# Up products of two SwiGLU layers: the two parts of an operand laid side by side, so that a third of the matmuls are twice as wide

## The chip, the cores and the metric

The kernel runs on one core of one Trainium2 chip. Its time is the device time of one launch in microseconds (us), and smaller is better. A launch computes the whole block for one sequence; the host only lays the arrays out.

## The reference, cut to what matters

The input is `x` of 512 tokens by 1024 features, in fp32. The block is a SwiGLU layer, a mixer, and another SwiGLU layer, each behind an RMS norm and each added to `x`:

```python
def swiglu(x, w_gu, w_down):
    g, u = jnp.split(x @ w_gu, 2, axis=-1)     # w_gu is 1024 x 5632
    return (jax.nn.silu(g) * u) @ w_down       # w_down is 2816 x 1024

x = x + 0.5 * swiglu(rmsnorm(x, norm_ffn1_g), ffn1_w_gu, ffn1_w_down)
x = x + hybrid_mixer(rmsnorm(x, norm_mix_g), ...)
x = x + 0.5 * swiglu(rmsnorm(x, norm_ffn2_g), ffn2_w_gu, ffn2_w_down)
return rmsnorm(x, final_norm_g)
```

The change concerns `x @ w_gu` (the up product) in both SwiGLU layers and nothing else of the arithmetic.

## The kernel before, in words

**Precision.** Every fp32 operand is split in a high part, which is the operand rounded to the type fp32r, and a low part, which is the rest. A product of two operands is the sum of three matmuls: high weights by high activations, high weights by low activations, low weights by high activations.

**Weights.** All weight blocks come from one flat array in the order `PLAN`; `STEPS` is the order in which they are used. `Weights.issue` handles one step: a cast on ScalarE makes the high part `wh` (L331), a subtraction on VectorE makes the low part `wl` (L332), and transfers that add in memory (`f<-f`, L309, issued by GpSimd) and one VectorE addition a set (L318) form sums of blocks for later steps. `wh` and `wl` have three buffers each. `take` issues two steps ahead of the product that runs.

**The up product in sets.** The up product of a layer gives 22 pieces of 128 columns of `g` and as many of `u`. The first four of each are done plainly (`mm_group`, `mm_single`, L380 and L366), and in each layer nine sets of seven products follow (`run_sets`, `Set.run`, L502). A set computes, with sums and differences of blocks (a Winograd scheme), a 2 by 2 block product with seven products instead of eight: its rows are the `g` and `u` columns, its columns are the two halves of 256 tokens (`HW`). The products are called m1, p2, q6, p5, q7, p4, p3. The order of two neighbouring sets s and t is written out in `order`: s.q6, s.p5, s.q7, t.m1, s.p4, t.p2, s.p3, t.q6 and so on. `Operands.make` splits the activation operand of each of the seven products once a layer, in 14 buffers of the pool `op`; its results stay for all nine sets.

**One product** is 24 matmuls: three terms, four 128-row pieces of the contraction, two 128-column pieces `e` of the weights. Each takes 128 x 128 weights and 256 columns of activations, and adds into one bank of PSUM of 512 fp32 a partition: columns 0 to 255 for `e` = 0, 256 to 511 for `e` = 1. A set has three banks: `b` takes m1, q6, q7, p4 one on top of the other; `a` starts as a copy of m1 (L507, ScalarE) and takes p2; `c` takes p5 and p3. After m1, q6 and q7 ScalarE copies the bank out (L510 for q6 and q7), and PE may go on adding to it when the copy is done; in the order above one other product always lies between. The results: after p2 a Silu of `a` (L727), after q7 `c` and the q7 copy together (L730), after p4 one half of the hidden tile (L734), after p3 `c` and the q6 copy (L739), Silu (L740) and the other half (L476).

**PSUM** has eight banks a core. Here six go round under the tag `mm`, two under `aux`. In the second SwiGLU layer `natural(i)` turns eight 128 x 512 pieces of `x`, one after the p3 of each of the first eight sets, with four 128 x 128 transposes on PE into an `aux` bank (L771) and a copy by ScalarE (L772).

**Order.** Which instruction stands where in an engine's queue is planned when the kernel is built, by priority (the program's order) and by when the planner takes an operand to be ready; at run time each engine goes through its queue in that order. Only the last stretch is scheduled by hand. After the sets `down_product` begins (`natural_set`, L625); its operands are split while the last sets run (L600, L601, L579, L583).

Of the kernel before, what the change touches and what calls it, by code (L numbers as in the profile page):

```python
# [12 lines left out]
ALU = mybir.AluOpType  # L13
# [166 lines left out]
def block_kernel(ctx: ExitStack, tc: tile.TileContext, xT, vecs, gf, gup, wgl, wts, out):  # L180
# [6 lines left out]
    ps = ctx.enter_context(tc.tile_pool(name="ps", bufs=6, space=bass.MemoryType.PSUM))  # L187
    pa = ctx.enter_context(tc.tile_pool(name="pa", bufs=2, space=bass.MemoryType.PSUM))

    cnt = [0]  # L190

# [10 lines left out]
    def tile_of(pool, shape, dtype=F32):  # L202
        cnt[0] += 1
        return pools[pool].tile(shape, dtype, tag=pool, name=f"{pool}{cnt[0]}")

    def T(dtype=F32):
        return tile_of("tp", [P, S], dtype)

    def MM():
        cnt[0] += 1  # L210
        return ps.tile([P, S], F32, tag="mm", name=f"mm{cnt[0]}")

    def AUX():
        cnt[0] += 1
        return pa.tile([P, S], F32, tag="aux", name=f"aux{cnt[0]}")


    ones = front.tile([P, P], F32, tag="ones", name="ones")
# [20 lines left out]
    class Weights:  # L239
# [239 lines left out]
    class Set:  # L479
# [34 lines left out]
        def first(self):  # L514
# [4 lines left out]
            nc.vector.tensor_tensor(out=t, in0=self.bank["a"], in1=self.v["m1"], op=ALU.add)  # L519
            return t  # L520

    class Operands:

        ORDER = ("m1", "p2", "p5", "q6", "q7", "p4", "p3")

        def __init__(self, b):
            self.b = b
            self.parts = {}  # L530
            self.sums = set()

# [19 lines left out]
        def make(self, p):  # L552
            if p in self.parts:
                return
            i = self.ORDER.index(p)
            if i > 0:
                self.make(self.ORDER[i - 1])
            v = self.sum(p)
            h, l = (tile_of("op", [P, 1024], F32R) for _ in range(2))
            hv, lv = (t.rearrange("p (k t) -> p k t", t=HW) for t in (h, l))  # L560
            nc.scalar.copy(hv, v)
            nc.vector.tensor_tensor(out=lv, in0=v, in1=hv.bitcast(F32), op=ALU.subtract)
            self.parts[p] = (h, l)
# [40 lines left out]
        def get(self, p):  # L604
            return self.parts[p]

    def natural_set(ops, banks, done, ahead=1):

        used = {"a"}
        for at, p in enumerate(SEQ):  # L610
            for q in SEQ[at : at + ahead + 1]:
                ops.make(q)
            n = {"m1": "b", "p2": "a", "q6": "b", "p5": "c", "q7": "b", "p4": "b", "p3": "c"}[p]
            fresh = n not in used
            used.add(n)
            o = banks[n]
            bh, bl = ops.get(p)
            for u in range(2):
                h, l = W.take()
                for j, (ww, aa) in enumerate(((h, bh), (h, bl), (l, bh))):  # L620
                    for i in range(2):
                        k = 2 * u + i
                        for t in range(2):
                            s = slice(k * HW + t * P, k * HW + (t + 1) * P)
                            nc.tensor.matmul(o[t], aa[:, s], ww[:, i * 512 : (i + 1) * 512],  # L625
                                             start=fresh and j == k == 0,
                                             stop=j == 2 and k == 3, skip_group_check=True)
            done(p, o)
# [21 lines left out]
    def ffn(up, down, norm, nxt, plain, at):  # L650
        xh, xl = norm.h, norm.l
        rows = []

        def finish(k):
            if k == at:
                rows.append(norm.finish())

        o = mm_group(up, KD, (0, DFF, P, DFF + P), xh, xl, extra=finish, slow=nxt is not None)
        row = rows[0]
        xn, xn_tile = {}, []  # L660

        def normed(j, l):

            if (j, l) not in xn:
                t = slice(l * HW, (l + 1) * HW)
                if not xn:
                    xn_tile.append(tile_of("hidw", [P, 4, 4, HW]))
                v = xn_tile[0][:, len(xn)]
                for i in range(4):
                    k = 4 * j + i  # L670
                    nc.vector.scalar_tensor_tensor(
                        out=v[:, i], in0=x[k][:, t],
                        scalar=vec[:, norm.goff + k : norm.goff + k + 1], in1=row[:, t],
                        op0=ALU.mult, op1=ALU.mult)
                xn[j, l] = v
            return xn[j, l]

        xo = Operands(normed)
# [36 lines left out]

        def down_operands(w):
            return DownOperands(
                lambda j, l: wides[w][:, 4 * j : 4 * j + 4, l * HW : (l + 1) * HW])

        def up_set(i):  # L720
            h = new_hid()

            def done(s, p):
                bank, v = s.bank, s.v
                if p == "p2":
                    s.g1 = T()
                    nc.scalar.activation(s.g1, s.first(), AF.Silu)  # L727
                if p == "q7":
                    u2 = T()
                    nc.vector.scalar_tensor_tensor(out=u2, in0=bank["c"], scalar=-1.0, in1=v["q7"],  # L730
                                                   op0=ALU.mult, op1=ALU.subtract)
                    s.u2 = u2
                if p == "p4":
                    nc.vector.scalar_tensor_tensor(  # L734
                        out=h[:, :, :HW], in0=pair(bank["b"]), scalar=-1.0, in1=pair(s.g1),
                        op0=ALU.mult, op1=ALU.mult)
                if p == "p3":
                    g2 = T()
                    nc.vector.tensor_tensor(out=g2, in0=bank["c"], in1=v["q6"], op=ALU.add)  # L739
                    nc.scalar.activation(g2, g2, AF.Silu)  # L740
                    mul(h[:, :, HW:], pair(s.u2), pair(g2))
                    if nxt is None and i < KD:
                        natural(i)
# [7 lines left out]
        def pair(t):  # L751
            return t.rearrange("p (e t) -> p e t", t=HW)

        run_sets(up_set)

        def split_hid(k):

            h, l = (tile_of("op", [P, 2, S], F32R) for _ in range(2))
            t = hid[k // 2]
            nc.scalar.copy(h, t)  # L760
            nc.vector.tensor_tensor(out=l, in0=t, in1=h.bitcast(F32), op=ALU.subtract)
            return h, l

        down_product(full(down, KF), split_hid, downs, nxt)

    def natural(i):

        X = XS[-1]
        o = AUX()
        for t in range(NTB):  # L770
            nc.tensor.transpose(o[:, t * P : (t + 1) * P], X[:, i, t * P : (t + 1) * P], ident)  # L771
        nc.scalar.copy(X[:, i], o)  # L772

    def down_product(us, split_hid, downs, nxt):
# [26 lines left out]
        A = [MM(), MM()]  # L801

        def run_wide(w):
            banks = {"a": A, "b": [(MM, AUX)[w % 2]() for _ in range(2)], "c": [MM(), MM()]}

            def done(p, o):
                for t in range(2):
# [10 lines left out]
                    elif p == "p3" and w < WIDE - 1:  # L818
                        add(0, 1, t, o[t], 0.5)

            natural_set(downs[w], banks, done)
            return banks["c"]

        for w in range(WIDE):
            C = run_wide(w)
# [728 lines left out]
```

## Time and profile before

| what | value |
|---|---|
| three runs | 1181.78, 1181.72, 1180.69 us; median 1181.72 |
| the profiled execution | 1180.99 us, of which 1179.3 us are the span of the trace |
| up products in sets, first layer | 50.15 to 231.58 us of the span |
| up products in sets, second layer | 878.47 to 1063.37 us |

The span is from the first to the last instruction of the trace; the profiled execution's own time is 1.7 us longer. Busy times of PE are modelled ends of pipelined matmuls, so what counts is the distance from one matmul's start to the next. PEld is the weight load of the same engine. In a group's row stand its count, its busy time, the mean of one in nanoseconds, then the idle time of the engine ahead of it and who ended that.

### The profile page before, as it was taken

The numbers are of one execution on the slowest core, as the hardware profiler recorded it, in microseconds if no ns is written. First come the engines' busy times: TensorE is split into PE (matmuls) and PEld (weight loads), VectorE is DVE, ScalarE is ACT, GpSimd is POOL, SyncE is SP. The second block draws the span as 40 slices with busy tenths as digits, with TensorE's granted clock in tenths as the row PEclk, the third lists the DMA queues.
The fourth block names the chain that finished last, engine by engine and source line by source line (L and its number), as shares of the span: only waits on it lengthen the run. The fifth ranks groups of instructions, "written<-read, shape, count | busy, mean of one in ns | idle before, by whom it ended". The sixth has DMA issues, their size and how long they took to land.

```text
span 1179.3 us, 19168 instructions
## 1 busy us (share of the span) xinstructions
PE 1170.9 (99%) x7794; PEld 1080.7 (92%) x7794; DVE 868.9 (74%) x1027; ACT 634.3 (54%) x790; POOL 117.4 (10%) x153
## 2 busy tenths in 40 slices
PE   9999999999999999999999999999999999999997
PEld 8899999988888889999999998998889999998886
DVE  7985656896568965767697787685598566579955
ACT  6564455674435655565565576544355554566543
POOL 0010101101010111100110100000001111001100
PEclk9999999999999999999999999999999999999999
DMA  9388777678524388777677766531638767757721
GB/s 350 79 210 197 171 193 178 158 199 206 212 85 113 87 207 223 189 180 200 180 196 192 199 199 186 141 109 44 232 68 211 181 180 175 190 153 186 178 83 72
DMA packets 62600, 200.25 MB, mean 170 GB/s; under 512 B 6864, under 2 KB 13136, under 8 KB 62512
## 3 DMA queue, kind: packets, MB, share of 16 engines
q0 software_dynamic: 18784, 68.17, 31.7%
q1 hardware_dynamic: 39088, 126.37, 30.9%
q10 hardware_dynamic: 4640, 4.49, 1.1%
q8 instruction: 61, 1.00, 0.3%
q14 instruction: 27, 0.22, 0.1%
HBM read 124.55 MB, written 8.39 MB: 113 GB/s over the span
## 4 chain that ended last, share of the span: by engine, by line
PE 97%; ACT 1%; issue 1%; DVE 1%; ACTq 0%; POOL 0%; POOLq 0%
PE mm L502 53%; PE mm L625 12%; PE mm L366 11%; PE mm L380 7%; PE mm L838 4%; PE aux L625 4%; PE aux L838 1%; PE aux L1161 1%; PE aux L1142 1%; PE aux L1120 1%; PE aux L1164 0%; PE aux L224 0%; PE aux L1121 0%; PE mm L857 0%; PE aux L771 0%
## 5 line engine op out<-in xcount | busy, mean ns | idle before, releaser
L331 ACT CAST wh<-f 128x1024 fp32r<-128x1024 f32 (+1 forms) x341 | 356.2, 1047 | 406.3 <-PE mm L502 207.4
L332 DVE TENSOR_TENSOR wl<-f,wh 128x1024 fp32r<-128x1024 f32 (+1 forms) x341 | 413.3, 1217 | 154.1 <-ACT wh L331 141.3
L502 PE MATMUL mm<-op,wh 128*128 128x256 f32 x3584 | 471.1, 284 | 0.4 <-ACT mm L507 0.4
L502 PEld LDWEIGHTS mm<-op,wh 128*128 128x128 f32 x3584 | 447.9, 192 | 2.2 <-ACT mm L507 0.8
L502 PE MATMUL mm<-op,wl 128*128 128x256 f32 x1792 | 251.5, 283 | 0.0
L502 PEld LDWEIGHTS mm<-op,wl 128*128 128x128 f32 x1792 | 231.2, 192 | 0.1
L309 POOL DMA_DIRECT2D f<-f x126 | 108.9, 869 | 929.0 <-DVE wl L332 542.2
L625 PE MATMUL mm<-wh,op 128*128 128x512 f32 x432 | 106.9, 389 | 0.0
L625 PEld LDWEIGHTS mm<-wh,op 128*128 128x128 f32 x432 | 80.9, 188 | 16.7
L366 PE MATMUL mm<-op,wh 128*128 128x512 f32 x384 | 91.0, 389 | 0.0
L366 PEld LDWEIGHTS mm<-op,wh 128*128 128x128 f32 x384 | 72.0, 188 | 14.9
L380 PE MATMUL mm<-op,wh 128*128 128x512 f32 x256 | 64.2, 393 | 0.0
L625 PE MATMUL mm<-wl,op 128*128 128x512 f32 x216 | 57.7, 389 | 0.0
L380 PEld LDWEIGHTS mm<-op,wh 128*128 128x128 f32 x256 | 48.1, 189 | 10.3
L318 DVE TENSOR_TENSOR f<-f,f 128x1024 f32<-128x1024 f32 x42 | 51.3, 1222 | 0.8
L625 PEld LDWEIGHTS mm<-wl,op 128*128 128x128 f32 x216 | 40.6, 188 | 8.4
L366 PE MATMUL mm<-op,wl 128*128 128x512 f32 x192 | 47.4, 389 | 0.0
L366 PEld LDWEIGHTS mm<-op,wl 128*128 128x128 f32 x192 | 36.0, 188 | 7.5
L510 ACT COPY tp<-mm 128x512 f32<-128x512 f32 x68 | 39.6, 583 | 0.0
L601 DVE TENSOR_TENSOR op<-hidw,op 128x1024 fp32r<-128x1024 f32 x28 | 34.0, 1219 | 1.1 <-ACT op L600 1.0
L380 PE MATMUL mm<-op,wl 128*128 128x512 f32 x128 | 34.3, 389 | 0.0
L416 ACT ACTIVATE op<-X,vec 128x512 fp32r<-128x512 f32 x23 | 16.5, 719 | 31.8 <-DVE X L859 24.3
(269 smaller groups left out, 1042.5 us busy)
## 6 DMA issues: line engine op xcount, KB each, us to landing
f<-wts SPq DMA_DIRECT2D x219, 512.0 KB, 4.5
f<-f POOLq DMA_DIRECT2D x126, 512.0 KB, 5.3
X<-xT SPq DMA_DIRECT2D x8, 256.0 KB, 5.3
xs<-X POOLq DMA_DIRECT2D x8, 256.0 KB, 2.3
ga<-tp ACTq DMA_DIRECT2D x8, 256.0 KB, 3.2
gb<-tp ACTq DMA_DIRECT2D x8, 256.0 KB, 4.7
tp<-ga SPq DMA_DIRECT2D x8, 256.0 KB, 4.3
y<-tp SPq DMA_DIRECT2D x7, 256.0 KB, 2.3
```

The source lines that it names most:

```text
L309: return nc.gpsimd.dma_start(out_, a, accum_op=ALU.add).ins
L318: nc.vector.tensor_tensor(out=s3, in0=a11, in1=a21, op=ALU.add)
L331: self.cast = nc.scalar.copy(h[:, :w], raw[:, :w]).ins
L332: nc.vector.tensor_tensor(out=l[:, :w], in0=raw[:, :w], in1=h[:, :w].bitcast(F32), op=ALU.subtract)
L366: nc.tensor.matmul(o, w[:, i * P : (i + 1) * P], a[k], start=j == k == 0, stop=j == 2 and k == kt - 1)
L380: nc.tensor.matmul(o[c], w[:, s : s + P], a[k], start=k == 0 and j == 0, stop=k == kt - 1 and j == 2)
L416: nc.scalar.activation(xh[k], x[k], AF.Copy, scale=g)
L502: nc.tensor.matmul(to, ww[:, s], aa[:, t], start=fresh and k == 0 and e == 0 and j == 0, stop=k == 3 and j == 2, skip_group_check=True)
L510: nc.scalar.copy(v, o)
L601: nc.vector.tensor_tensor(out=lv, in0=v, in1=hv.bitcast(F32), op=ALU.subtract)
L625: nc.tensor.matmul(o[t], aa[:, s], ww[:, i * 512 : (i + 1) * 512], start=fresh and j == k == 0, stop=j == 2 and k == 3, skip_group_check=True)
L838: nc.tensor.matmul(o[t][e], b if j == 1 else a, wl if j == 2 else wh, start=k == K0 and e == 1 and j == 0, stop=k == KF - 1 and j == 2, sk ...
```

## The change

Seven of the nine sets of each layer (all but the first and the last) run a product as 8 wide matmuls (high weights by 512 columns: the high and the low part of the activations side by side) and then 8 narrow ones (low weights by the high part, 256 columns). The wide result needs a bank for each `e`, so each accumulator is a pair of banks: the left halves hold high x high plus low x high, the right halves hold high x low, and the sum of left and right is formed when the result is taken out. The first and the last set run the 24 narrow matmuls as before, in the first bank of their pairs.

- `Both` replaces the split of `Operands.make` in the two SwiGLU layers: the same two buffers an operand, filled by two copies and two subtractions of 128 x 512 rather than one each of 128 x 1024.
- `PairSet` replaces `Set` for the up products. The copies out of a pair: after m1 one copy of both banks to `a` (128 x 1024); after q6 and q7 two copies of 128 x 512 on ScalarE and one addition on VectorE; `onto` is two additions on VectorE where there was one; `whole` is a copy on ScalarE and an addition on VectorE, used after p2 (`a`) and p4 (`b`), where there was none.
- PSUM is four pairs with fixed names while the sets run: `x` for every `a`, and `w`, `z`, `y` in turn for `b` and `c`. `banks` closes the six and two banks before the sets and opens them again behind them.
- The transposes of `natural` move from behind p3 to behind p5, into the pair `x`. They are issued as matmuls with the transpose flag, with `start` on the first of four only.
- The sets of the mixer keep `Set` and its banks.

```diff
+    def banks(paired=False):
+        stage.close()
+        for n, b in (("pairs", 1),) if paired else (("mm", 6), ("aux", 2)):
+            cnt[0] += 1
+            pools[n] = stage.enter_context(tc.tile_pool(
+                name=f"{n}{cnt[0]}", bufs=b, space=bass.MemoryType.PSUM, reuse_waits="tile"))
...
+    class Both:
+        def __init__(self, v):
+            self.t = []
+            for i in range(2):
+                t = tile_of("op", [P, 2, 2, HW], F32R)
+                w = v[:, 2 * i : 2 * i + 2]
+                nc.scalar.copy(t[:, :, 0], w)
+                nc.vector.tensor_tensor(out=t[:, :, 1], in0=w, in1=t[:, :, 0].bitcast(F32),
+                                        op=ALU.subtract)
...
+    class PairSet:
+        BANK = {"m1": "b", "p2": "a", "q6": "b", "p5": "c", "q7": "b", "p4": "b", "p3": "c"}
+        def __init__(self, group_, done, i, merged):
...
+            self.tags = {"a": "x", "b": "wzy"[i % 3], "c": "ywz"[i % 3]}
...
+            def product(to, ww, aa):
+                nonlocal first
+                for k in range(4):
+                    for e in range(2):
+                        nc.tensor.matmul(to(e), ww[:, k * HW + e * P : k * HW + (e + 1) * P],
+                                         aa(k), start=first and k == 0 and (self.merged or e == 0),
+                                         stop=k == 3 and ww is l, skip_group_check=True)
+                first = False
+            if self.merged:
+                product(lambda e: o[:, e], h, x_.both)
+                product(lambda e: o[:, e, :HW], l, x_.high)
+            else:
+                half = self.flat(n)
+                for ww, aa in ((h, x_.high), (h, x_.low), (l, x_.high)):
+                    product(lambda e: half[:, e * HW : (e + 1) * HW], ww, aa)
+            if p == "m1" and self.forked:
+                a = self.open("a")
+                if self.merged:
+                    nc.scalar.copy(a, o)
+                else:
+                    nc.scalar.copy(a[:, 0], o[:, 0])
+            elif p in ("m1", "q6", "q7"):
+                self.taken(p, n)
...
+        def taken(self, p, n):
...
+            nc.scalar.copy(pair(v), self.left(n))
+            nc.scalar.copy(pair(r), self.right(n))
+            nc.vector.tensor_tensor(out=v, in0=v, in1=r, op=ALU.add)
+        def onto(self, n, t):
...
+            for part in (self.left(n), self.right(n)):
+                nc.vector.tensor_tensor(out=pair(t), in0=part, in1=pair(t), op=ALU.add)
+        def whole(self, n):
...
+            nc.scalar.copy(pair(t), self.right(n))
+            nc.vector.tensor_tensor(out=pair(t), in0=self.left(n), in1=pair(t), op=ALU.add)
...
             def done(s, p):
                 if p == "p2":
+                    if s.forked:
+                        g = s.whole("a")
+                        s.g1 = g if s.merged else T()
+                    else:
+                        s.g1 = g = s.m1
+                        s.onto("a", g)
+                    nc.scalar.activation(s.g1, g, AF.Silu)
+                if p == "p5" and nxt is None and i < KD:
+                    natural(i, MM2("x")[:, 0])
                 if p == "q7":
+                    s.onto("c", s.q7)
                 if p == "p4":
+                    t = s.whole("b")
                     nc.vector.scalar_tensor_tensor(out=h[:, :, :HW], in0=pair(t), ...)
                 if p == "p3":
+                    s.onto("c", s.q6)
+                    nc.scalar.activation(s.q6, s.q6, AF.Silu)
+                    nc.vector.scalar_tensor_tensor(out=h[:, :, HW:], in0=pair(s.q7), ...)
...
-            return Set(xo, done)
+            return PairSet(xo, done, i, i not in (0, (KF - plain) // 2 - 1))
+        banks(paired=True)
         run_sets(up_set)
+        banks()
...
-    def natural(i):
+    def natural(i, o):
         X = XS[-1]
-        o = AUX()
         for t in range(NTB):
-            nc.tensor.transpose(o[:, t * P : (t + 1) * P], X[:, i, t * P : (t + 1) * P], ident)
+            b = slice(t * P, (t + 1) * P)
+            nc.tensor.matmul(o[:, b], X[:, i, b], ident, start=t == 0, stop=t == NTB - 1,
+                             is_transpose=True, skip_group_check=True)
         nc.scalar.copy(X[:, i], o)
```

More of the change, by code (lines that the diff above doesn't have):

```diff
@@ L520, in first, with high, low, both @@
             return t
+    class Both:
[7 more added lines that the diff above has]
+                                        op=ALU.subtract)
+                self.t.append(t)
+        def high(self, k):
+            return self.t[k // 2][:, k % 2, 0]
+        def low(self, k):
+            return self.t[k // 2][:, k % 2, 1]
+        def both(self, k):
+            return self.t[k // 2][:, k % 2].rearrange("p a t -> p (a t)")
@@ new lines, in pair, with left, right, open @@
+    def pair(t):
+        return t.rearrange("p (e t) -> p e t", t=HW)
+    class PairSet:
+        BANK = {"m1": "b", "p2": "a", "q6": "b", "p5": "c", "q7": "b", "p4": "b", "p3": "c"}
+        def __init__(self, group_, done, i, merged):
+            self.merged = merged
+            self.group = group_
+            self.done = done
+            self.tags = {"a": "x", "b": "wzy"[i % 3], "c": "ywz"[i % 3]}
+            self.bank = {}
+        def left(self, n):
+            return self.bank[n][:, :, :HW]
+        def right(self, n):
+            return self.bank[n][:, :, HW:]
+        def open(self, n):
+            self.bank[n] = MM2(self.tags[n])
+            return self.bank[n]
+        def run(self, p):
+            n = self.BANK[p]
+            fresh = n not in self.bank
+            o = self.open(n) if fresh else self.bank[n]
+            x_ = self.group.get(p)
+            h, l = W.take()
+            first = fresh
+            def product(to, ww, aa):
[21 more added lines that the diff above has]
+                self.taken(p, n)
+            self.done(self, p)
+        def flat(self, n):
+            return self.bank[n][:, 0]
+        def taken(self, p, n):
+            v = T()
+            setattr(self, p, v)
+            if not self.merged:
+                nc.scalar.copy(v, self.flat(n))
+                return
+            r = T()
+            nc.scalar.copy(pair(v), self.left(n))
+            nc.scalar.copy(pair(r), self.right(n))
+            nc.vector.tensor_tensor(out=v, in0=v, in1=r, op=ALU.add)
+        def onto(self, n, t):
+            if not self.merged:
+                nc.vector.tensor_tensor(out=t, in0=self.flat(n), in1=t, op=ALU.add)
+                return
+            for part in (self.left(n), self.right(n)):
+                nc.vector.tensor_tensor(out=pair(t), in0=part, in1=pair(t), op=ALU.add)
+        def whole(self, n):
+            if not self.merged:
+                return self.flat(n)
+            t = T()
+            nc.scalar.copy(pair(t), self.right(n))
+            nc.vector.tensor_tensor(out=pair(t), in0=self.left(n), in1=pair(t), op=ALU.add)
+            return t
@@ L605, in get, with natural_set @@
             return self.parts[p]
-    def natural_set(ops, banks, done, ahead=1):
+    def natural_set(ops, bank, done, ahead=1):
         used = {"a"}
@@ L615, in natural_set @@
             used.add(n)
-            o = banks[n]
+            o = bank[n]
             bh, bl = ops.get(p)
@@ L676, in normed @@
             return xn[j, l]
-        xo = Operands(normed)
+        xo = Operands(normed, Both)
         hid = []
@@ L803, in run_wide @@
         def run_wide(w):
-            banks = {"a": A, "b": [(MM, AUX)[w % 2]() for _ in range(2)], "c": [MM(), MM()]}
+            bank = {"a": A, "b": [(MM, AUX)[w % 2]() for _ in range(2)], "c": [MM(), MM()]}
             def done(p, o):
@@ L819, in done @@
                         add(0, 1, t, o[t], 0.5)
-            natural_set(downs[w], banks, done)
-            return banks["c"]
+            natural_set(downs[w], bank, done)
+            return bank["c"]
         for w in range(WIDE):
```

39 lines of the change are left out of this document (18 added, 21 removed).

## The prediction

> **What bounds the kernel now.** I read the head of the page first, then the chain that ended last, then the up products by stretch, and at the end the order of single instructions there. The page:
>
> ```profile
> span 1179.3 us, 19168 instructions
> PE 1170.9 (99%) x7794; PEld 1080.7 (92%) x7794; DVE 868.9 (74%) x1027; ACT 634.3 (54%) x790; POOL 117.4 (10%) x153
> PEclk9999999999999999999999999999999999999999
> PE mm L502 53%; PE mm L625 12%; PE mm L366 11%; PE mm L380 7%; PE mm L838 4%; PE aux L625 4%; PE aux L838 1%; PE aux L1161 1%; PE aux L1142 1%; PE aux L1120 1%; PE aux L1164 0%; PE aux L224 0%; PE aux L1121 0%; PE mm L857 0%; PE aux L771 0%
> L502 PE MATMUL mm<-op,wh 128*128 128x256 f32 x3584 | 471.1, 284 | 0.4 <-ACT mm L507 0.4
> ```
>
> PE is busy throughout, at its full granted clock, and the sets (L502) are 53% of the chain with 0.4 us of idle time over the whole run. The chain in order of time shows the pace of the two shapes:
>
> ```profile
> 28.39 21.76 PE mm L366 x96
> 50.15 181.43 PE mm L502 x1512
> 231.58 38.11 PE mm L625 x168
> ...
> 878.47 25.92 PE mm L502 x216
> 904.82 20.16 PE mm L502 x168
> 1046.10 17.27 PE mm L502 x144
> ```
>
> A 256-column matmul takes 181.43 / 1512 = 120.0 ns, a 512-column one 21.76 / 96 = 226.7 ns. So the first layer's nine sets run back to back, at 20.16 us a set and 2.88 us a product. The 256 further columns cost 106.7 ns; what is left of the narrow matmul, 120.0 - 106.7 = 13.3 ns, is paid for each instruction whatever its width.
>
> **The change part by part.** *PE.* A merged product is 8 wide and 8 narrow matmuls: 8 x 226.7 + 8 x 120.0 = 2773 ns, against 24 x 120.0 = 2880. It saves 107 ns, which is eight times those 13.3 ns. Seven sets of seven products in two layers are 98 merged products: 98 x 0.1067 = 10.5 us, all of it on the chain. A set goes from 20.16 to 19.41 us, so 0.75 us a set is what everything else may eat before nothing is left.
>
> The page TensorE: Matmul & The Clock Gate of the Trainium skill, section Back-to-back issue gap, gives warm matmuls as N / 2.4 + 2.5 ns, that is about 109 and 216 ns. By it the fixed part is 2.5 ns, the saving an estimated 8 x 2.5 = 20 ns a product and 2 us in all. The trace disagrees: 13.3 ns.
>
> *VectorE and ScalarE.* A steady set of the first layer, and the groups in it:
>
> ```profile
> 107.58:127.74 20.16, 20.16 (x171) 20.16 (x170) 12.20 (x12) 10.02 (x13) 2.57 (x3) 1.00 0.76 183
> L331 ACT CAST wh<-f 128x1024 fp32r<-128x1024 f32 x8 | 8.4, 1048 | 10.8 <-PE mm L502 9.5 <-issue 1.3
> L510 ACT COPY tp<-mm 128x512 f32<-128x512 f32 x2 | 1.2, 584 | 0.0
> L507 ACT COPY mm<-mm 128x512 f32<-128x512 f32 x1 | 0.6, 575 | 0.0
> L332 DVE TENSOR_TENSOR wl<-f,wh 128x1024 fp32r<-128x1024 f32 x7 | 8.6, 1223 | 4.9 <-ACT wh L331 4.9
> L318 DVE TENSOR_TENSOR f<-f,f 128x1024 f32<-128x1024 f32 x1 | 1.2, 1225 | 0.0
> L739 DVE TENSOR_TENSOR tp<-mm,tp 128x512 f32<-128x512 f32 x1 | 0.7, 693 | 1.5 <-PE mm L502 1.5
> L740 ACT ACTIVATE tp<-tp 128x512 f32<-128x512 f32 x1 | 0.6, 637 | 0.6 <-DVE tp L739 0.6
> ```
>
> A merged set adds six 128x512 additions on VectorE (one behind q6, one behind q7, one more `onto` at q7 and at p3, one `whole` at p2 and at p4): 6 x 0.69 = 4.1 us, so 12.2 becomes 16.3 of 19.41 us. ScalarE gains four copies of 0.58 and a longer m1 copy. That copy, 128x1024 out of PSUM, is not in the trace: bounds 0.58 (one L507) and 1.17 (two); I take 1.05, the cast of that size. So 10.0 becomes 10.0 + 2.3 + 0.5 = 12.8 of 19.4 us. Neither engine becomes the bound; what counts is the hand-over of a pair to PE.
>
> *The hand-over inside a set.* PE adds again to a pair after m1, q6 and q7, one product later each time, and waits for ScalarE's copies only, not for the additions. The order of instructions at a p3 and the q6 behind it:
>
> ```profile
> 115.26 1.12 PE L502 MATMUL mm<-op,wl 128*128 128x256 f32 x8
> 115.46 1.05 ACT L331 CAST wh<-f 128x1024 fp32r<-128x1024 f32 x1 [1.26 <-PE mm L502]
> 116.10 1.99 PEld L502 LDWEIGHTS mm<-op,wh 128*128 128x128 f32 x16
> 116.42 0.69 DVE L739 TENSOR_TENSOR tp<-mm,tp 128x512 f32<-128x512 f32 x1 [1.54 <-PE mm L502]
> 117.03 1.22 DVE L332 TENSOR_TENSOR wl<-f,wh 128x1024 fp32r<-128x1024 f32 x1
> 117.14 0.64 ACT L740 ACTIVATE tp<-tp 128x512 f32<-128x512 f32 x1 [0.64 <-DVE tp L739]
> 118.38 1.05 ACT L331 CAST wh<-f 128x1024 fp32r<-128x1024 f32 x1 [0.60 <-PE mm L502]
> 119.34 0.58 ACT L510 COPY tp<-mm 128x512 f32<-128x512 f32 x1
> ```
>
> The cast starts 0.2 us behind a product's last high matmul, and 0.96 us (8 x 120.0) of that product are then left, so it ends 0.2 + 1.05 - 0.96 = 0.3 us behind the product. Two copies of 0.58 behind it end at 1.5 us; PE comes back 2.77 us behind the product, which leaves 1.3 us. A Silu in front (0.64) leaves 0.7. The m1 copy: 0.3 + 1.05 = 1.35, the same. So I take 0. The uses by another set have room: `b` of s after p4, `c` after p3 and `x` after p2 are opened again three products later, 8.3 us, against a copy, an addition and what stands ahead of them. The next thing late would be the weights; the cast above runs for the product three later, because it waits for the third-last `wh`, and so has two products of slack.
>
> *Into the pairs and out of them.* The first pair `w` has to take over banks of the six, which may still hold the last plain results:
>
> ```profile
> 49.51 0.69 DVE L476 TENSOR_TENSOR tp<-mm,row 128x512 f32<-128x512 f32 x1
> 49.98 2.08 PE L502 MATMUL mm<-op,wh 128*128 128x256 f32 x16
> 51.24 0.69 DVE L476 TENSOR_TENSOR tp<-mm,row 128x512 f32<-128x512 f32 x1
> ...
> 878.31 2.08 PE L502 MATMUL mm<-op,wh 128*128 128x256 f32 x16
> 879.53 0.68 DVE L476 TENSOR_TENSOR tp<-mm,row 128x512 f32<-128x512 f32 x1
> ...
> 230.42 0.68 DVE L734 SCALAR_TENSOR_TENSOR hid<-mm,tp 128x512 f32<-128x512 f32 x1
> 231.42 2.00 PE L625 MATMUL mm<-wh,op 128*128 128x512 f32 x8
> ```
>
> Before, m1 at 49.98 got a bank that had long been free. The last two plain results leave their banks at 49.51 + 0.69 = 50.20 and 51.24 + 0.69 = 51.93 us. Counted through, the plain results go round the six banks so that in the first layer the earlier of the two lies in the lowest bank and the later in the highest; if pairs are laid out from the lowest in order of use, `w` waits for the earlier only: 0.3 us. Bounds: 0 and, waiting for the later, 1.9 us. In the second layer the same count puts neither under `w`: 0, with a bound of 879.53 + 0.68 - 878.31 = 1.9. On the way out the down product opens the bank of the last set's p4, which VectorE left at 231.10, 0.3 us before that product began: 0, bound 1.2 (one more `wl` ahead of it). Were that cover gone everywhere, it would be 2 x 1.9 + 2 x 1.2 = 6.2 us.
>
> *The rest.* `Both` makes two halves of an operand rather than one piece: 2 x 0.69 - 1.22 = 0.16 us more of VectorE an operand, seven a layer, 1.1 us while VectorE is full at the start of a layer. The tightest one is q7's in the second layer:
>
> ```profile
> 889.27 1.22 DVE L562 TENSOR_TENSOR op<-hidw,op 128x1024 fp32r<-128x1024 f32 x1
> 889.82 2.08 PE L502 MATMUL mm<-op,wh 128*128 128x256 f32 x16
> 904.39 0.44 PE aux L771 x4
> ```
>
> The low part is there at 890.49 and wanted 0.96 us into the product, at 890.78; that covers 0.3 us, two operands' worth. I take 0, bound 0.8. The four transposes cost 0.44 us of PE a set wherever they stand; behind p5 `x` is free since p2, three products back, and their copy has q7 and t.m1 to finish before `x` is opened again: 0. SP's and GpSimd's transfers are the same ones; VectorE frees `wl` and the blocks later within a product, which the two products of slack cover.
>
> *Sum.* -10.5 + 0.3 = -10.2 us. The profiled execution, 1180.99 (span 1179.3 and 1.7 outside), becomes 1170.8; it lies 0.7 us under the median of the runs shown, so by that it is 1171.5. I say 1171.2.
>
> **The rivals.** *ScalarE gets stuck behind VectorE (slower).* If the planned queues put the Silu of p3 ahead of the cast and the copies, and VectorE's `wl` (1.22) and block addition (1.22) ahead of the two additions it needs (1.38), the Silu ends 0.2 + 3.82 + 0.64 = 4.7 us behind p3, the cast at 5.7, the two q6 copies at 6.9. PE wants the pair 5.54 us behind p3, and waits 1.3 us a set: 14 x (1.3 - 0.75) = +7.7, 1189. With `wl` alone ahead it is 0.12 us a set, 1.7 in all, and 1172.5. It turns slower at 0.75 us a set. For it speaks that q7 and p3 now bring 1.22 + 3 x 0.69 = 3.3 us of VectorE in 2.77; against it that in the rows above VectorE takes the result (116.42) before the next `wl` (117.03), and the cast (115.46) goes before the Silu, so the plan does not follow the program's order. Chance 0.12, a third of it within 0.2%.
> The same page of the Trainium skill, in its table of specifications, has the queues of ScalarE and VectorE as strict FIFO: what is planned wrongly isn't mended at run time. The trace agrees in so far as a `wl` ready at 116.51 (115.46 + 1.05) starts at 117.03 behind L739.
>
> *The hand-overs at the ends cost in full*, 6.2 us: 1180.99 - 10.5 + 6.2 = 1176.7. Chance 0.12. *Some sets lose 0.1 to 0.5 us* because queues are fuller: 14 x 0.3 = 4.2 us, 1175. Chance 0.08.
> *The change doesn't save what it says*, because matmuls that alternate in width run at another pace than either alone, or the fixed part goes to the narrow ones alone: between nothing and a fifth of the 10.5 us, 1179 to 1181. Against it: at 231.58 narrow gives way to wide with no gap. Chance 0.04.
>
> **How the numbers follow.** Forecast 0.64, by itself 1170 to 1173. The range, 1169.8 to 1178.0, takes in the ends and partial stalls and leaves out the slower case and no saving. A measurement of this kernel tells 0.2%, 2.4 us, from no change: faster (under 1179.4) holds the forecast, the ends, the partial stalls, 0.84, of which I take off 0.03 for stalls larger than reckoned, same 0.08, slower 0.11.
>
> **What would show it.** Wide matmuls at 226.7 and narrow at 120.0 ns in L502's place; set starts 19.4 us apart, 19.85 with transposes; 7794 - 784 = 7010 matmuls; VectorE near 930 us and ScalarE near 675 us busy; no idle time of PE put down to a ScalarE copy. It is wrong if PE waits at q7, p4 or p2 in each merged set, or for microseconds at the first m1 or the first down product.

## The result and the profile after

The changed kernel takes 1173.99 us (median of six runs, 1173.48 to 1174.98) against 1181.68 (six runs, 1180.69 to 1181.78): the ratio is 0.9938, interval 0.9926 to 0.9951. It is 7.7 us faster; 10.2 were forecast. The head of the page, the longest parts of its chain, and PE's waits:

```profile
span 1172.0 us, 17786 instructions
PE 1163.1 (99%) x7010; PEld 1038.9 (89%) x7010; DVE 922.0 (79%) x1125; ACT 668.5 (57%) x860; POOL 117.1 (10%) x153
PE mm L517 22%; PE mm L757 13%; PE mm L381 9%; PE y L596 9%; PE w L596 9%; PE z L596 9%; PE mm L395 7%; PE x L596 4%; PE mm L974 4%; PE aux L757 4%; PE aux L974 1%; PE aux L1297 1%; PE aux L1278 1%; PE aux L1256 1%; DVE wl L347 0%
```

```profile
PE aux L239 <- POOL ones L236: 1.1, 1, 1.1
PE w L596 <- DVE tp L491: 0.5, 1, 0.5
PE mm L517 <- ACT mm L522: 0.4, 2, 0.2
```

784 matmuls are gone, and PE is still the chain. Its only new wait is the second row, 0.5 us once, at the first m1. Some products of the chain in order of time (those left out are marked), and three stretches by engine (busy us and counts of PE, PEld, VectorE, ScalarE, GpSimd; the first is one merged set, the others are the sets of the two layers):

```profile
50.59 3.10 PE w L596 x24
...
68.00 2.88 PE w L596 x24
70.88 2.79 PE x L596 x16
...
98.90 2.79 PE z L596 x16
101.70 2.79 PE y L596 x16
...
228.00 38.11 PE mm L757 x168
```

```profile
107.12:126.67 19.55, 19.55 (x114) 17.20 (x113) 15.98 (x19) 12.28 (x17) 2.56 (x3) 1.00 0.76 189
50.59:227.84 177.25, 177.25 (x1120) 160.82 (x1121) 151.99 (x170) 113.80 (x149) 23.78 (x28) 1.00 0.76 185
874.93:1055.68 180.75, 180.75 (x1154) 164.25 (x1152) 152.27 (x170) 118.06 (x157) 23.56 (x28) 1.00 0.75 183
```

A merged product takes 2.793 us (19.55 / 7), not 2.773, and a set 19.55 us, not 19.41. PE is busy without a gap in both layers' sets. Here is where the span went, from the starts of the matmuls that open each stretch, for all runs of the study:

| kernel | to the first m1 | sets 1 | to the sets of layer 2 | sets 2 | from there to the last matmul |
|---|---|---|---|---|---|
| before | 49.98 | 181.43 | 646.89 | 184.90 | 108.83 |
| changed | 50.59 | 177.25 | 647.09 | 180.75 | 109.06 |
| changed, again (e9) | 50.97 | 177.25 | 647.13 | 180.74 | 109.47 |
| 24 narrow in pairs (e2) | 51.96 | 181.50 | 647.27 | 185.86 | 110.03 |
| two and two (e3) | 50.40 | 176.93 | 646.85 | 180.37 | 109.05 |
| VectorE doubled (e4) | 50.71 | 177.27 | 649.89 | 180.74 | 111.25 |
| one and one (e6) | 50.53 | 179.31 | 646.77 | 181.15 | 109.57 |
| aux first (e7) | 49.98 | 177.63 | 647.11 | 180.75 | 109.07 |
| all sets merged (e8) | 50.72 | 178.72 | 649.50 | 182.06 | 113.00 |
| alternate (e10) | 50.09 | 177.16 | 646.85 | 180.36 | 109.45 |
| two and two, aux first (e11) | 50.41 | 177.32 | 647.90 | 180.37 | 109.04 |
| ScalarE held (e12) | 50.92 | 184.64 | 647.99 | 187.39 | 110.38 |

The sets gain 4.2 us in each layer; 0.6 go at the first m1 and 0.4 in the stretches that the change does not touch. These vary by as much: the last one differs by 0.4 us between the two executions of the changed kernel, and the matmuls just ahead of the sets start between 0.3 us early and 1.3 us late (e2) against before. So a row of this table is read by its sets. The m1 itself can be told apart: it starts 0.9 us behind the last matmul ahead of it in the changed kernel, against 0.23 before, so it costs 0.7 us.

One run of e3 took 1634.90 us at a granted clock of 0.655 and is left out of its time below.

### The profile page after: what moved, and what is told of

Same layout as the page of the kernel before. It is cut to its first block, busy times and chain, and to the rows that moved or that the text cites. A ratio compares the mean times of both kernels' runs of the same rounds, so it can differ in the third digit from the quotient of the medians.

```text
span 1172.0 us, 17786 instructions
## 1 busy us (share of the span) xinstructions
PE 1163.1 (99%) x7010; PEld 1038.9 (89%) x7010; DVE 922.0 (79%) x1125; ACT 668.5 (57%) x860; POOL 117.1 (10%) x153
## 4 chain that ended last, share of the span: by engine, by line
PE 95%; DVE 2%; ACT 2%; issue 1%; ACTq 0%; POOL 0%; POOLq 0%
PE mm L517 22%; PE mm L757 13%; PE mm L381 9%; PE y L596 9%; PE w L596 9%; PE z L596 9%; PE mm L395 7%; PE x L596 4%; PE mm L974 4%; PE aux L757 4%; PE aux L974 1%; PE aux L1297 1%; PE aux L1278 1%; PE aux L1256 1%; DVE wl L347 0%
## 5 line engine op out<-in xcount | busy, mean ns | idle before, releaser
L517 PE MATMUL mm<-op,wh 128*128 128x256 f32 x1568 | 208.1, 285 | 0.4 <-ACT mm L522 0.4
L517 PEld LDWEIGHTS mm<-op,wh 128*128 128x128 f32 x1568 | 196.9, 191 | 2.1 <-ACT mm L522 0.8
L517 PE MATMUL mm<-op,wl 128*128 128x256 f32 x784 | 110.0, 283 | 0.0
L517 PEld LDWEIGHTS mm<-op,wl 128*128 128x128 f32 x784 | 101.2, 192 | 0.1
L381 PEld LDWEIGHTS mm<-op,wh 128*128 128x128 f32 x384 | 72.0, 188 | 15.0
L596 PE MATMUL w<-op,wh 128*128 128x512 f32 (+1 forms) x352 | 73.1, 353 | 0.5 <-DVE tp L491 0.5
L596 PE MATMUL y<-op,wh 128*128 128x512 f32 (+1 forms) x384 | 73.3, 338 | 0.0
L596 PE MATMUL z<-op,wh 128*128 128x512 f32 (+1 forms) x320 | 72.7, 371 | 0.0
L596 PEld LDWEIGHTS y<-op,wh 128*128 128x128 f32 x384 | 58.4, 190 | 6.2
L596 PEld LDWEIGHTS w<-op,wh 128*128 128x128 f32 x352 | 56.2, 190 | 8.2 <-issue 0.9
L596 PEld LDWEIGHTS z<-op,wh 128*128 128x128 f32 x320 | 54.0, 189 | 8.2
L395 PEld LDWEIGHTS mm<-op,wh 128*128 128x128 f32 x256 | 47.8, 188 | 10.3
```

What stands on the lines that cost most here:

```text
L381: nc.tensor.matmul(o, w[:, i * P : (i + 1) * P], a[k], start=j == k == 0, stop=j == 2 and k == kt - 1)
L395: nc.tensor.matmul(o[c], w[:, s : s + P], a[k], start=k == 0 and j == 0, stop=k == kt - 1 and j == 2)
L517: nc.tensor.matmul(to, ww[:, s], aa[:, t], start=fresh and k == 0 and e == 0 and j == 0, stop=k == 3 and j == 2, skip_group_check=True)
L596: nc.tensor.matmul(to(e), ww[:, k * HW + e * P : k * HW + (e + 1) * P], aa(k), start=first and k == 0 and (self.merged or e == 0), stop=k ...
```

## The experiments

Two things were to be settled: why a merged product takes 20 ns more than its parts, and whether the added work is hidden or only nearly so. Theory: the 20 ns are paid on PE where the width of its matmuls changes (a border), and outside PE the change costs nothing. Rival: the copies, additions and hand-overs of the pairs take them.

**e1, widths alone.** A new kernel with nothing but matmul streams, each with its own pattern:

```diff
...
+    plans = [("pa", [W] * 16, 6), ("pb", [N] * 24, 8), ("pc", ([W] * 8 + [N] * 8), 10),
+             ("pd", ([W] * 16 + [N] * 16), 5)]
...
+    plans2 = [("pa", ([W] * 2 + [N] * 2), 40), ("pc", [W, W, N, N, N, N], 20),
+              ("pd", ([W] * 8 + [N] * 2), 16)]
...
```

> A stream of matmuls alone: no weights cast, no evacuation while it runs; seven patterns of wide (512 columns, W) and narrow (256, N) matmuls, everything else of the block left out. Theory 1 (the border): the 20 ns that a merged product takes over 8 x 226.7 + 8 x 120.0 belong to the borders between widths on PE, as the gaps 233, 236, 228, 233, 231 behind the narrow matmuls at 231.42 us of the kernel before suggest. Then W alone paces at 226.7 ns and N alone at 120.0; 8W8N takes 2793 ns a round, 16W16N 5567 (one pair of borders in twice the matmuls), and 8W2N shows a border too. For 2W2N it leaves two outcomes: 20 ns at every border pair (713 ns a round) or less, if five wide ones are needed to pay in full. Rival (the surroundings): ScalarE's and VectorE's reads of PSUM at the start of a product slow the wide ones; then the stream alone paces at 226.7 and 120.0 throughout and 8W8N takes 2773.

PE in order of time: where each stream starts, with its count of matmuls.

```profile
9.33 24.75 PE L199 MATMUL pa<-x,w 128*128 128x512 f32 x96 [9.33 <-ACT x L189]
33.91 23.20 PE L199 MATMUL pb<-x,w 128*128 128x256 f32 x192
56.95 28.10 PE L199 MATMUL pc<-x,w 128*128 128x512 f32 x160
84.88 28.00 PE L199 MATMUL pd<-x,w 128*128 128x512 f32 x160
112.71 28.03 PE L199 MATMUL pa<-x,w 128*128 128x512 f32 x160
140.58 18.83 PE L199 MATMUL pc<-x,w 128*128 128x512 f32 x120
159.25 33.34 PE L199 MATMUL pd<-x,w 128*128 128x512 f32 x160
```

W is a wide matmul and N a narrow one. From start to start: wide alone settle at 226.7 ns (the first thirteen of that stream are slower, most of them 427 ns apart), narrow alone take 23.04 us / 192 = 120.0 ns. 8W8N takes 27.93 / 10 = 2.793 us a round, the kernel's own figure, with no other engine at work but VectorE for two copies, 1.3 of these 27.9 us. 16W16N takes 27.83 / 5 = 5.57, one surcharge for twice the matmuls; 2W2N 27.87 / 40 = 0.697, 3 ns over; 2W4N 18.67 / 20 = 0.933, nothing over. Taken singly, in the stream as in the kernel, the starts lie 233, 236, 228, 233, 231 and then 227 ns apart behind narrow ones, and 113, 119, then 120 behind wide ones: +27 and -7, 20 ns a round. That is shown: the surcharge is PE's and comes from how the widths follow one another. The surroundings are ruled out.

**e3, two wide and two narrow in turn**

```diff
-                product(lambda e: o[:, e], h, x_.both)
-                product(lambda e: o[:, e, :HW], l, x_.high)
+                for k in range(4):
+                    for to, ww, aa in ((lambda e: o[:, e], h, x_.both),
+                                       (lambda e: o[:, e, :HW], l, x_.high)):
+                        for e in range(2):
+                            nc.tensor.matmul(to(e), ww[...], aa(k), ...)
```

> The changed kernel with wide and narrow matmuls mixed finer: two wide, two narrow, for each of the four pieces of the contraction, so four borders of each kind a product instead of one. If each border pair costs 20 ns whatever its length: products of 2773 + 80 = 2853 ns, 98 x 0.06 = 5.9 us more than the changed kernel, 1180. If the surcharge is a debt that narrow matmuls build up and the wide ones pay off: products near 2793 ns or under, 1174. If the surroundings slow the first wide ones of a product: 2793 too, but with long gaps only at the product's start.

1172.64 us (three runs), ratio 0.9925 (0.9909 to 0.9942). Four times as many borders, and the sets are shorter, by 0.3 and 0.4 us, as 2W2N had it. So it is not a fixed price for a border; this mixture with short runs pays less.

**e5 and e6, finer mixtures, alone and in the kernel**

```diff
...
+    plans = [("pa", [W, N], 80), ("pb", [W, N, N], 40), ("pc", [W] * 4 + [N] * 4, 20), ("pd", [W, W, N], 40)]
+    plans2 = [("pa", [W, N, N, W], 40), ("pc", [W] * 8 + [N] * 4, 12), ("pd", [W] * 8 + [N] * 16, 8)]
...
```

> The stream of matmuls alone again, with finer mixtures (all else of the block left out). In the first stream a wide one behind narrow ones took 233, 236, 228, 233, 231 and then 227 ns, a narrow one behind wide ones 113 and then 119 and 120; 2W2N came to 696.7 ns a round (3.3 over 2 x 226.7 + 2 x 120.0) and 2W4N to 933.3 (0 over). Theory (a lead that wide matmuls build up over five and narrow ones use up over two): the surcharge falls with the length of the wide run, so 1W1N about 347 ns (0 over), 4W4N between 1387 and 1407 (up to 20 over), 8W4N and 8W16N 20 over. Rival (a price for each change of width): 1W1N 20 over, 367.

The starts of the streams in the chain of that run, in order of time:

```profile
9.90 29.84 PE pa L199 x160
39.74 18.70 PE pb L199 x120
58.43 28.05 PE pc L199 x160
86.48 23.47 PE pd L199 x120
109.96 27.87 PE pa L199 x160
```

4W4N comes to 28.05 / 20 = 1.403 us, 16 over, and 8W4N and 8W16N took 20 over, as expected. 1W2N is 18.70 / 40 = 0.467, 1 over; 2W1N is 23.47 / 40 = 0.587, 13 over. The last row, one wide, two narrow, one wide, is 2W2N once more: 27.87 / 40 = 0.697, 3 over. 1W1N starts slowly too; from its later rounds (three pairs take 1060 ns) it is 0.353 a round, 7 over: neither the 0 of the theory nor the 20 of the rival. In e6 the kernel's products are one wide and one narrow in turn:

```diff
+                for k in range(4):
+                    for e in range(2):
+                        s = slice(k * HW + e * P, k * HW + (e + 1) * P)
+                        nc.tensor.matmul(o[:, e], h[:, s], x_.both(k), ...)
+                        nc.tensor.matmul(o[:, e, :HW], l[:, s], x_.high(k), ...)
```

> The changed kernel with one wide and one narrow matmul in turn, 8 of each a product. If the surcharge of a border is a lead built up by runs of wide ones: products at 2773 ns, all of the predicted 107 ns saved, 98 x 0.020 = 2.0 us less than the changed kernel, 1172.0 us (the mixture of two and two gave 1172.8). If it is a price for a change of width: products of 2773 + 8 x 20 = 2933, over 1187.

1176.36 us, ratio 0.9957 (0.9945 to 0.9970), slower than the changed kernel. In the first layer's sets three pairs take 241 + 120 + 236 + 113 + 233 + 117 = 1060 ns against 1040, as in the stream, and a merged product takes 2819 to 2832 ns. But in the second layer 18 of the 49 merged products run at 230 and 117 ns in turn and take 2773 to 2777 ns, nothing over. So the same order of the same widths has two paces in one kernel; the sets lose 2.1 us in the first layer (0.4 of it is a new wait in its first set) and 0.4 in the second against the changed kernel's. The idea of a lead that wide runs build up and narrow ones use up does not explain this end. What stands is a table from the streams (surcharge in ns a round): 8W with 2, 4, 8 or 16 N 20, 4W4N 16, 2W2N 3, 1W2N 1, 2W4N 0, 2W1N 13, 1W1N 7. The cheapest have at most two wide ones in a row and at least two narrow ones behind. Why stays open.

**e10 and e11, can it be had for nothing?** e10 turns the order round in every other product (`terms.reverse()` when the last product ended narrow), so that runs are 16 long; e11 is e3's mixture; both lay the aux banks out first, as e7 below. e9 is the changed kernel beside them.

> The changed kernel itself, on the same chip as the three beside it: 1174.0 us (1173.5 to 1175.0), for them to be compared with.

> The changed kernel with the order of wide and narrow matmuls turned round in every other merged product, so that runs are 16 long and a border pair comes once in two products, and with the aux banks laid out first. In the stream alone 16W16N cost 20 ns over per 32 matmuls, so a product should take 2783 instead of 2793 ns: 98 x 0.010 = 1.0 us less, and 0.2 from the banks, 1172.8. If a product that starts with its low weights has to wait for them (the low part is made behind the high one), PE waits for wl in every other product, and it is over 1174.

> The mixture of two wide and two narrow, with the aux banks laid out first. In the stream alone 2W2N was 3.3 ns over, so a product takes 2787 at most, in the mixture's own trace a little less: 98 x 0.007 = 0.7 us or more under the changed kernel, 0.2 from the banks: 1172.5 to 1173.1.

e9 1174.2 (0.9938; 0.9926 to 0.9951), e10 1173.94 (0.9937; 0.9924 to 0.9951), e11 1173.98 (0.9933; 0.9921 to 0.9946). The traces have nearly the expected gain in layer 2's sets (180.36 and 180.37 against 180.74), and in e10's first layer a merged product takes 2784 ns on average, where 2783 was expected; but in the times it can't be told from nothing: the runs of one kernel lie 1 to 3 us apart. No version of this study beats the changed kernel by more than its measurement tells.

**e2, pairs with 24 narrow matmuls**

```diff
-                product(lambda e: o[:, e], h, x_.both)
-                product(lambda e: o[:, e, :HW], l, x_.high)
+                for to, ww, aa in ((lambda e: o[:, e, :HW], h, x_.high),
+                                   (lambda e: o[:, e, HW:], h, x_.low),
+                                   (lambda e: o[:, e, :HW], l, x_.high)):
+                    product(to, ww, aa)
```

> The changed kernel with its pairs, its second halves, its added copies and additions and its moved transposes, but each product in 24 narrow matmuls again (high by high to the left half, high by low to the right). Theory (all added work outside PE is hidden, and what the change brings is PE's alone): products at 2.88 us, so 98 x 0.087 = 8.5 us come back, about 1182.5 us, within 0.2% of the kernel before, with the wait at the first m1 (0.5 us) and nothing else. Rival (pairs and evacuation bring or cost something by themselves): outside 1180 to 1185.

1183.89 us, ratio 1.0019 (1.0009 to 1.0028): 1.4 over the expected 1182.5. The first layer's sets take 181.50 us against 181.43 before, so all evacuation there is hidden at that pace. In the second layer PE waits once, in the last set (at 1060.73, in front of p4): the copy behind q7 stands behind a weight cast on ScalarE.

```profile
PE y L596 <- ACT tp L628: 0.7, 1, 0.7
PE w L596 <- DVE tp L491: 0.5, 1, 0.5
```

The second row is the wait at the first m1 again. The execution that left this trace is the slowest of the ten (1185.56); 1.3 us of its first stretch lie ahead of anything that the edit touches. With the gain of the wide matmuls taken away the change is a small loss, 2.3 us by the medians, and what it brings is PE's alone.

**e4, VectorE loaded.** A maximum of a tile with itself behind each of q6, q7, `onto` and `whole` in the merged sets. It was described as eight a set; `onto` got one, not two, so it is six, and the expected load by distances is 8 x 1.13 + 16 x 0.60 = 18.6 us a set, not 19.8.

```diff
+    def again(t):
+        nc.vector.tensor_tensor(out=t, in0=t, in1=t, op=ALU.max)
...
             nc.vector.tensor_tensor(out=v, in0=v, in1=r, op=ALU.add)
+            again(v)
...
```

> The changed kernel with a second VectorE instruction (maximum of a tile with itself, 128x512) behind every addition of q6, q7, onto and whole in the merged sets: eight more a set (one behind each of the two additions of an onto). By durations VectorE would have 16.3 + 8 x 0.69 = 21.8 us in a set of 19.55 and would set the pace: 14 x 2.3 = 32 us more, 1206. By distances from start to start (1.13 for 1024 elements, 0.60 for 512) it has 8 x 1.13 + 18 x 0.60 = 19.8 us, just over the set: 14 x 0.3 = 4 us more, 1178, and more where Silu and copies come late. If the hand-over to PE hangs on ScalarE alone and ScalarE isn't held up: under 1180. If VectorE's lateness holds up ScalarE's queue (the slower rival of the prediction): PE idle in front of q7, p2 or p4 in each merged set, and over 1185.

1177.04 us, ratio 0.9966 (0.9955 to 0.9977). The sets by engine:

```profile
50.71:227.98 177.27, 177.27 (x1121) 160.86 (x1122) 172.07 (x210) 114.08 (x149) 22.81 (x28) 1.00 0.75 185
877.86:1058.61 180.75, 180.75 (x1154) 164.25 (x1152) 174.45 (x210) 118.55 (x157) 22.82 (x27) 1.00 0.75 182
```

VectorE is busy 172 of 177 us and PE loses nothing: PE hangs on ScalarE's copies, and this load of VectorE, which by distances still fits into the set, does not reach them. The 3 us that the kernel is slower come behind the sets, in both down products and in the mixer (2.8 and 2.2 us in the table, whose execution took 1178.89); how they get there was not followed up.

**e12, ScalarE held at the hand-over**

```diff
             nc.scalar.copy(pair(r), self.right(n))
+            for _ in range(4 if p == "q6" else 0):
+                nc.scalar.copy(pair(r), self.right(n))
```

> The changed kernel with four more copies of 128x512 on ScalarE behind the two that hand the pair back after q6 (merged sets). By the prediction's reckoning the copies end 1.5 us behind the product and PE comes back at 2.79, so 1.3 us are free; four more take 4 x 0.49 to 4 x 0.58 = 2.0 to 2.3 us, and PE should wait 0.7 to 1.0 us at q7 in each merged set: 14 x 0.7 to 1.0 = 10 to 14 us, 1184 to 1188. If PE doesn't wait for these copies (the hand-over is looser than reckoned): 1174. If the slack was used up already (copies end later than 1.5 us): 2 us a set, 1202.

1189.87 us, ratio 1.0069 (1.0056 to 1.0083): 15.7 us over the changed kernel (e9). The sets are 7.4 and 6.6 us longer, 14.0 / 14 = 1.0 us a set, the upper end of what was expected. So PE does hang on these copies. How much time was free it does not show cleanly, because the planned queues came out in another order. Around one q7 (the pair `y`; L632 are the held copies):

```profile
102.04 1.05 ACT L346 CAST wh<-f 128x1024 fp32r<-128x1024 f32 x1
102.99 1.83 ACT L632 COPY tp<-y 128x512 f32<-128x512 f32 x3
104.87 2.11 PE L596 MATMUL y<-op,wh 128*128 128x512 f32 x8
107.77 0.76 PE L596 MATMUL w<-op,wl 128*128 128x256 f32 x5
108.45 0.59 ACT L630 COPY tp<-y 128x512 f32<-128x512 f32 x1
109.10 2.14 PE L596 MATMUL y<-op,wh 128*128 128x512 f32 x8 [0.57 <-ACT tp L630]
```

A cast got in between the held copies, and 11 of the 16 matmuls of the next product (`w`) now stand ahead of q7, the other 5 behind it. So PE fills most of the wait for the held copies, and then p4 comes so soon behind q7 that it waits for q7's ordinary copies (L630). The longest waits of PE in the run are of this kind, a row for each of the three pairs; the first of them:

```profile
PE y L596 <- ACT tp L630: 2.0, 4, 0.6
```

**e7, aux banks first**

```diff
-        for n, b in (("pairs", 1),) if paired else (("mm", 6), ("aux", 2)):
+        for n, b in (("pairs", 1),) if paired else (("aux", 2), ("mm", 6))[::(1, -1)[cnt[0] > 0]]:
```

> The changed kernel with the two aux banks laid out below the six at the start, so that the first pair w takes over banks that have long been free. Theory (the first m1 waited 0.5 us for the evacuation of the last plain gate result but one): that wait is gone, the first stretch ends 0.4 to 0.7 us sooner, 1173.4 us. Rival (the first m1 is late because VectorE is full and its operands or weights are late): PE begins at the same place, and another wait stands there.

1173.81 us, ratio 0.9934 (0.9920 to 0.9947). PE's wait for VectorE is gone and the first m1 starts at 49.98, as before the change; but the first set is 0.4 us longer, with a new wait on the weight load in front of q7 (61.78), behind the copy of q6 (61.15 to 61.73):

```profile
PEld w L596 <- ACT tp L626: 0.3, 1, 0.3
```

Most of the 0.6 us is lost again four products later.

**e8, the first and last set merged too**

```diff
-            return PairSet(xo, done, i, i not in (0, (KF - plain) // 2 - 1))
+            return PairSet(xo, done, i, True)
```

> The changed kernel with the first and the last set merged too: 28 more products at 2.79 us. If all added work is hidden there as well: 28 x 0.087 = 2.4 us less, 1171.6 us. If VectorE, which is full at both ends of a layer, makes a hand-over late (operands of the first set, the down product's operands beside the last): PE waits of 0.5 to 2 us at the first p4, q7 or at the first down product in each layer, and 1173 to 1177 us.

1183.51 us, ratio 1.0016 (1.0007 to 1.0025), 9.5 us over the changed kernel and worse than either expectation. PE's waits:

```profile
PE w L596 <- DVE op L546: 2.1, 2, 1.1
PE z L596 <- DVE tp L639: 1.5, 2, 0.8
PE mm L757 <- ACT wh L346: 1.3, 3, 0.6
PE mm L757 <- ACT mm L945: 0.6, 2, 0.3
```

At the start PE waits for the first set's operands (first row), at the end, in front of the last p3, for the additions that take the last set's results out of its bank (second row) and, in the down product, for weights and a copy that came late. By the table the sets lose 1.5 and 1.3 us where 1.2 each were to be won, the stretches behind them 2.4 and 3.9.

## Why the prediction was right, and where it was off

**The sign, the place and the mechanism held.** The fixed part of a matmul is paid 8 times fewer a product, PE stays the chain, and 7010 matmuls, 922 us of VectorE and 668.5 of ScalarE are near what was forecast (7010, 930, 675). The Trainium skill's page TensorE: Matmul & The Clock Gate (section Back-to-back issue gap) gives N / 2.4 + 2.5 ns for the isolated gap of a warm matmul. Taken for this stream it would have saved an estimated 2 us; the 7.7 measured and e1's streams (120.0 ns a narrow one) speak against that here.

**The term that was mis-sized is PE's**: 98 x 0.107 = 10.5 us took a product as the sum of its parts. It saves 2.880 - 2.793 = 0.087 us, 98 x 0.087 = 8.5; the missing 2.0 us are the border's 20 ns, shown alone in e1. The prediction named widths in alternation as a rival and dismissed it because narrow gives way to wide "with no gap" at 231 us. The rows were there in the trace of before, had they been measured:

```profile
231.42 2.00 PE L625 MATMUL mm<-wh,op 128*128 128x512 f32 x8
233.26 1.07 PE L625 MATMUL mm<-wl,op 128*128 128x512 f32 x4
234.16 1.98 PE L625 MATMUL mm<-wh,op 128*128 128x512 f32 x8
235.98 0.84 PE L625 MATMUL mm<-wl,op 128*128 128x512 f32 x3
```

Eight wide ones behind narrow ones take 1.84 us to the next start, eight behind wide ones 1.82. No gap means that nothing waited, not that the pace is the same.

**The hand-over inside a set**, taken as 0: right, and its working nearly so. In the changed kernel, around one q6 (the pair `w`, product until 118.29):

```profile
115.70 0.69 DVE L639 TENSOR_TENSOR tp<-z,tp 128x512 f32<-128x512 f32 x1 [0.83 <-PE z L596]
116.31 1.22 DVE L347 TENSOR_TENSOR wl<-f,wh 128x1024 fp32r<-128x1024 f32 x1
117.44 0.69 DVE L639 TENSOR_TENSOR tp<-z,tp 128x512 f32<-128x512 f32 x1
117.58 1.05 ACT L346 CAST wh<-f 128x1024 fp32r<-128x1024 f32 x1 [1.26 <-issue]
118.29 2.00 PE L596 MATMUL y<-op,wh 128*128 128x512 f32 x8
118.54 0.63 ACT L875 ACTIVATE tp<-tp 128x512 f32<-128x512 f32 x1
119.07 0.57 ACT L629 COPY tp<-w 128x512 f32<-128x512 f32 x1
119.53 0.59 ACT L630 COPY tp<-w 128x512 f32<-128x512 f32 x1
121.09 2.00 PE L596 MATMUL w<-op,wh 128*128 128x512 f32 x8
126.87 1.01 ACT L611 COPY x<-z 128x1024 f32<-128x1024 f32 x1
```

The Silu does stand in front, the copies end at 120.12, 1.8 us behind the product, and PE is back at 121.09: 1.0 us free, where 1.3 and, with a Silu, 0.7 were reckoned. e12 shows that PE waits once these copies end late enough. The m1 copy takes 1.01 (1.05 taken). VectorE's 16.3 us a set are 16.0.

**The slower rival** (ScalarE stuck behind VectorE) did not come. In the rows above VectorE makes the first of the two additions that the Silu needs ahead of the next low part (115.70) and the second behind it (117.44), so one low part does stand between. But that addition ends at 118.13, while ScalarE is in the cast until the Silu begins at 118.54. Even 172 of 177 us of VectorE in e4 did not bring a wait of PE in the sets. At the ends of a layer, where operands are made beside the sets, VectorE does hold PE up in e8 (2.1 and 1.5 us), through late operands and through additions that hand a bank back; whether ScalarE's queue has a part in it is not shown.

**The ends.** The first m1 waits for the earlier plain result as worked out, but it costs 0.7 us (0.5 of it idle time of PE) where 0.3 was taken: VectorE leaves the bank at 50.44, 0.24 us later than before, and PE begins 0.15 us after that; the second layer's first m1 and both ways out cost nothing measurable, as taken. The operand halves of `Both` cost nothing in sets of the changed kernel; the late hand-over of e2, 0.7 us, was a copy behind a cast. Another 0.4 us of the gap are in stretches without a change.

## What to carry to other kernels

A matmul's fixed part can be read off two widths in one trace, and merging narrow ones into wide ones wins just that part times their number; but measure a border between the widths too, by start-to-start distances, before multiplying. In steady sets the copies that hand a PSUM bank back decide, not the load of the engine that adds up later: find the free time between the last copy and PE's return. Where operands are still being made, that free time is gone, and the same edit loses (e8).

## What the runs showed of the hardware

PE's pace depends on how widths follow one another: in streams of eight wide and eight narrow matmuls the first five of 512 columns take 233, 236, 228, 233 and 231 ns instead of 227, and the first of 256 behind them takes 113 instead of 120, with almost nothing else running. Two and two cost 3 ns over their parts, one and one 7 (and nothing in some products of e6), eight and eight 20. The cause was not found.
